# Second feed-forward product in seven block products instead of eight, with 512-column weight tiles and squares on ScalarE

## Chip, cores and metric

The kernel runs on one core of one Trainium2 chip. The metric is the device time of one execution in microseconds (us). The engines are TensorE (PE; its weight loads have a row of their own, PEld), VectorE (DVE), ScalarE (ACT), GpSimd (POOL) and SyncE (SP), the last of which issues most DMA transfers.

## The reference, cut to what matters

A decoder trunk of two layers: 512 tokens plus 16 meta tokens, model width 1024. Each layer is a token mixer (stick-breaking attention, latent attention and retention, joined by one output projection), a layer norm, a feed-forward block and another layer norm:

```python
def squared_relu_mlp(h, w1, w2):
    return jnp.square(jax.nn.relu(h @ w1)) @ w2
...
    for l in range(DEPTH):
        mix = hybrid_mixer(...)
        h = layer_norm(DN_ALPHA * h + mix, ln1_g[l], ln1_b[l])
        h = layer_norm(DN_ALPHA * h + squared_relu_mlp(h, w_ff1[l], w_ff2[l]), ln2_g[l], ln2_b[l])
    return h[:, N_PAD + N_META:]
```

w1 is 1024 x 4096 and w2 is 4096 x 1024, all in float32. The last layer needs only the 512 tokens.

## The kernel before, in words

Activations lie feature-major: a tile has 128 features on the partitions and the tokens on the free axis, 528 tokens in the first layer (layer 0) and 512 in the second (layer 1). Every float32 operand of a product is split into a high part, rounded to the type fp32r by a copy on ScalarE, and a low part, the rest, by a subtraction on VectorE. A 128-deep slice of a product is three matmuls: high x high, high x low, low x high (`proj`, line 554). So an output tile of 128 features over a depth of 1024 takes 24 matmuls for each group of tokens. `groups` (line 563) gives two groups, of 256 and 272 tokens, in layer 0 and one of 512 in layer 1; around layer norms both layers use two halves.

Weights come by `wload` (line 537): one DMA on SP brings 512 KB (128 x 1024) into a raw tile, ScalarE copies it to the high tile and VectorE subtracts to the low tile, in pieces of 512 columns. All three are tiles of one pool W, of ten tiles of 1024 columns (line 436). Other working tiles are units of 528 columns, 63 of them. PSUM has eight banks, shared by two streams of the program.

The feed-forward block (`layer`, from line 1320) works through the 4096 hidden features in four quarters of 1024. In a quarter, `ff1` (line 1324) makes eight tiles of hidden features: product, relu on ScalarE, square on VectorE (which reads PSUM and the relu), split. Then `ff2` (line 1338) makes eight output tiles from those eight hidden ones, and `accum` (line 1238) adds each from PSUM into the running sum r on VectorE; in the first quarter it also brings in the scaled residual, in two instructions. In a layer 24 of the 32 `ff2` output tiles lie in the first three quarters.

At two places in each layer the work is arranged so that a layer norm lies beside matmuls: the last four weights of the mixer's output projection (`nw=4`) and of the last quarter's `ff2` (`nf=4`) are all loaded and held, the first half of the tokens is finished with all of them, and while the second half is multiplied with the same weights the layer norm of the first half runs (`ln_group`, line 639).

The order of the work is not that of the code. All operations are recorded with a rank (`nc.rank`), and a planner (`schedule`, line 314) places them one at a time at the earliest start that its fixed costs give; ties go by rank and then by the order of recording. Each engine then runs its list strictly in that order. A tile of a pool can be given out only when all earlier ones of its stream still fit (`fits`, line 187).

Of the kernel before, what the change touches and what calls it, by code (L numbers as in the profile page):

```python
# [8 lines left out]
F32 = mybir.dt.float32  # L9
F32R = mybir.dt.float32r  # L10
# [5 lines left out]
P = 128  # L16
# [28 lines left out]
def f32(ap):  # L45
    return ap.bitcast(F32)
# [381 lines left out]
class Builder:  # L428
    def __init__(self, ctx, tc, a):
        self.tc, self.a = tc, a  # L430
        self.nc = Recorder(tc.nc)
        self.sb = ctx.enter_context(tc.tile_pool(name="sb", bufs=1))
        self.psp = ctx.enter_context(tc.tile_pool(name="ps", bufs=1, space=bass.MemoryType.PSUM))
        ka, km = PR['KA'], PR['KM']
        self.U = Pool(self.sb, "u", NT, 63).stream(63)
        self.W = Pool(self.sb, "w", 1024, 10).stream(10)
        self.VC = Pool(self.sb, "v", 1280, 3).stream(3)
        self.TC = Pool(self.sb, "t", 48, 12).stream(12)
        ps = Pool(self.psp, "ps", 512, 8)
        self.PA, self.PM = ps.stream(ka), ps.stream(km)  # L440
        self.PP = self.PA
# [95 lines left out]
    def wload(self, src, eng=None):  # L537
        nc = self.nc
        n = src.shape[1]
        raw = self.W.tile([P, 1024], F32)  # L540
        with nc.rank(nc.cur + PR['wd']):
            nc.sync.dma_start(raw[:, :n], src)
        wh = self.W.tile([P, 1024], F32R)
        wl = self.W.tile([P, 1024], F32R)
        with nc.rank(nc.cur + PR['wl']):
            for c in range(0, n, PR['wa']):
                e = min(n, c + PR['wa'])
                nc.scalar.copy(wh[:, c:e], raw[:, c:e])
            for c in range(0, n, PR['wc']):
                e = min(n, c + PR['wc'])  # L550
                (eng or nc.vector).tensor_sub(wl[:, c:e], raw[:, c:e], f32(wh[:, c:e]))
        return wh, wl

    def proj(self, out, w, b0, rhs, c0, c1):
        wh, wl = w
        n = len(rhs)
        for i, (h, l) in enumerate(rhs):
            s = slice((b0 + i) * P, (b0 + i + 1) * P)
            self.mm(out, wh[:, s], h[:, c0:c1], i == 0, False)
            self.mm(out, wh[:, s], l[:, c0:c1], False, False)  # L560
            self.mm(out, wl[:, s], h[:, c0:c1], False, i == n - 1)

    def groups(self, full):
        return self.halves(True) if full else [(0, NX)]
# [22 lines left out]
    def norm_tokens(self, src, xn, n, final=False):  # L587

        nc = self.nc
        st = self.small(16)  # L590
        nc.vector.bn_stats(st[:n, 0:6], src[0])
        nc.vector.bn_stats(st[:n, 6:12], src[1])
        nc.vector.bn_aggr(st[:n, 12:14], st[:n, 0:12])
        self.rstd(st[:n, 14:15], st[:n, 13:14], n)
        if final:
            for i in range(2):
                s = slice(512 * i, 512 * i + 512)
                nc.vector.scalar_tensor_tensor(out=xn[i], in0=src[i], scalar=st[:n, 12:13], in1=self.fg[:n, s],
                                               op0=ALU.subtract, op1=ALU.mult)
                nc.vector.scalar_tensor_tensor(out=xn[i], in0=xn[i], scalar=st[:n, 14:15], in1=self.fb[:n, s],  # L600
                                               op0=ALU.mult, op1=ALU.add)
            return
        nc.vector.scalar_tensor_tensor(out=st[:n, 15:16], in0=st[:n, 12:13], scalar=-1.0, in1=st[:n, 14:15],
                                       op0=ALU.mult, op1=ALU.mult)
        nc.scalar.activation(xn[0], src[0], AF.Identity, bias=st[:n, 15:16], scale=st[:n, 14:15])
        nc.vector.tensor_scalar(out=xn[1], in0=src[1], scalar1=st[:n, 12:13], scalar2=st[:n, 14:15],
                                op0=ALU.subtract, op1=ALU.mult)
# [640 lines left out]
    def layer(self, l, h, first):  # L1248
# [69 lines left out]

        r_mix, r = r, [None] * KT
        nf = PR['nf']  # L1320
        for qd in range(4):
            us, ws3 = [], {}

            def ff1(mt, c0, c1):
                n = c1 - c0
                if mt not in ws3:
                    ws3[mt] = self.wload(self.a["wff1"][l, 8 * qd + mt])
                    us.append((self.unit(F32R), self.unit(F32R)))
                u = us[mt]
                ps = self.mmb()  # L1330
                self.proj(ps[:, :n], ws3[mt], 0, h, c0, c1)
                rl = self.unit()[:, :n]
                nc.scalar.activation(rl, ps[:, :n], AF.Relu)
                sq = self.unit()[:, :n]
                nc.vector.scalar_tensor_tensor(out=sq, in0=ps[:, :n], scalar=0.0, in1=rl, op0=ALU.max, op1=ALU.mult)
                self.split(u[0][:, c0:c1], u[1][:, c0:c1], sq, "a")

            def ff2(mt, w, c0, c1):
                n = c1 - c0
                ps = self.mmb()  # L1340
                self.proj(ps[:, :n], w, 0, us, c0, c1)
                self.accum(ps[:, :n], r[mt][:, c0:c1], h[mt] if qd == 0 else None, c0, c1)

            head = PR['head'] if qd == 0 else 0
            for mt in range(head):
                ff1(mt, *gs[0])
            if qd == 0:
                with nc.rank(R + 23):
                    self.ln_group(r_mix, 1 + 2 * l, hn, *gs[1], False)
            for mt in range(head):  # L1350
                ff1(mt, *gs[1])
            for mt in range(head, 8):
                for g in gl:
                    ff1(mt, *g)
            for mt in range(8 if qd < 3 else 8 - nf):
                w = self.wload(self.a["wff2"][l, qd, mt])
                if qd == 0:
                    r[mt] = self.unit()
                for g in gl:
                    ff2(mt, w, *g)  # L1360
        final = l == DEPTH - 1
        ws = {mt: self.wload(self.a["wff2"][l, 3, mt]) for mt in range(8 - nf, 8)}
        for i, g in enumerate(gs):
            with nc.rank(R + 30 + 2 * i):
                for mt in range(8 - nf, 8):
                    ff2(mt, ws[mt], *g)
        if final:
            self.fg = self.W.tile([P, 1024], F32)
            self.fb = self.W.tile([P, 1024], F32)
            nc.sync.dma_start(self.fg, self.a["fgb"][:, 0:1024])  # L1370
            nc.sync.dma_start(self.fb, self.a["fgb"][:, 1024:2048])
        hn = None if final else self.new_h()
        with nc.rank(R + 31):
            self.ln_group(r, 2, hn, *gs[0], final)
# [117 lines left out]
def _arrays(x, meta_tokens, ln_emb_g, ln_emb_b, w_in, mla_q_norm, mla_kv_norm, w_uq, w_ukv, w_out,  # L1492
            ln1_g, ln1_b, w_ff1, w_ff2, ln2_g, ln2_b):
    A = lambda v: np.asarray(v)
    d = _tables()
    d["xm"] = np.concatenate([A(x)[0][::-1], A(meta_tokens)[::-1]], 0)

    def chunks(w, tiles):

        L, K = w.shape[:2]  # L1500
        v = w[:, :, tiles.reshape(-1)].reshape(L, K // P, P, tiles.shape[0], P)
        return np.ascontiguousarray(v.transpose(0, 3, 2, 1, 4)).reshape(L, tiles.shape[0], P, K)

    d["win"] = chunks(A(w_in), _win_cols())
    uq = chunks(A(w_uq), _uq_cols().reshape(8, P)).reshape(DEPTH, 4, 2, P, 384)
    d["wuq"] = uq.transpose(0, 1, 3, 2, 4).reshape(DEPTH, 4, P, 768)
    ukv = chunks(A(w_ukv), _ukv_cols().reshape(8, P)).reshape(DEPTH, 4, 2, P, 256)
    d["wukv"] = ukv.transpose(0, 1, 3, 2, 4).reshape(DEPTH, 4, P, 512)
    wo = A(w_out).reshape(DEPTH, 3, 4, P, 4, 2, P)
    d["wout"] = wo[:, [0, 2, 1]].transpose(0, 1, 4, 3, 5, 2, 6).reshape(DEPTH, 3, 4, P, 1024)  # L1510
    d["wff1"] = chunks(A(w_ff1), np.arange(D_FF).reshape(32, P))
    f2 = A(w_ff2).reshape(DEPTH, 4, 8, P, 8, P)
    d["wff2"] = f2.transpose(0, 1, 4, 3, 2, 5).reshape(DEPTH, 4, 8, P, 1024)
    col = lambda v: A(v).reshape(-1, P).T
    sets = [(ln_emb_g, ln_emb_b), (A(ln1_g)[0], A(ln1_b)[0]), (A(ln2_g)[0], A(ln2_b)[0]), (A(ln1_g)[1], A(ln1_b)[1])]
    sm = [np.concatenate([col(g), col(b)], 1) for g, b in sets]
    for l in range(DEPTH):
        sm += [col(A(mla_q_norm)[l]), col(A(mla_kv_norm)[l])]
    d["csmall"] = np.concatenate(sm, 1)
    d["fgb"] = np.broadcast_to(np.concatenate([A(ln2_g)[1], A(ln2_b)[1]])[None], (P, 2048))  # L1520
    return {n: np.ascontiguousarray(v) for n, v in d.items()}
# [16 lines left out]
```

## Time and profile before

| | us |
|---|---|
| median of 3 runs (1598.54 to 1599.52) | 1598.9 |
| profiled execution, its own time | 1599.59 |
| its span, first to last instruction | 1597.6 |

The profile is of one execution. Busy time of PE is that of matmuls that overlap each other, so it says that PE had work, not how fast it went; the rate is read from counts of matmuls in a stretch. Mean durations of single instructions hold a latency that the next instruction overlaps, so the rate of an engine is read from stretches in which instructions follow each other without a gap. All instructions have one line (416), since the planner issues them all from there; they are told apart by tiles (u: working units, w: weights, ps: PSUM, t: small ones).

### The profile page before, as it was taken

The page shows a single profiled execution, that of the slowest core. Times are in us where ns is not written, and L with a number is a line of the kernel's source. Part 1 is how long each engine was busy: PE and PEld are TensorE (multiplying, and loading weights), DVE is VectorE, ACT ScalarE, POOL GpSimd, SP SyncE. Part 2 cuts the span into 40 slices and gives each one's busy share as a digit, 9 for nine tenths or more (in the row PEclk, how much of TensorE's full clock was granted, in tenths as well). Part 3 has the DMA queues.
Part 4 walks back from the last instruction along what each step waited for, and adds up shares of the span by engine and source line. Part 5 has one row for each costly group of instructions (what it writes and reads, how often), then busy time and mean ns, then how long its engine had stood idle before and what let it go on. Part 6 is the DMA issues. An engine that isn't in the chain of part 4 may idle for free.

```text
span 1597.6 us, 27869 instructions
## 1 busy us (share of the span) xinstructions
PE 1564.4 (98%) x10842; PEld 1454.4 (91%) x10842; DVE 1038.0 (65%) x2549; ACT 768.2 (48%) x1787; POOL 103.7 (6%) x201
## 2 busy tenths in 40 slices
PE   6999999999999999999999999999999999999997
PEld 6999999988999999999999999988889888888887
DVE  7777777899784443434467767869998544344445
ACT  5664744588553241423336666545885414232330
POOL 5112100110000000000002112001000000000000
PEclk9999999999999999999999999999999999999999
DMA  5423422312122222222224223323112332223332
GB/s 201 111 72 110 128 74 77 93 59 61 52 82 94 93 93 89 85 92 93 93 67 133 84 77 106 115 78 113 57 55 66 107 100 97 92 93 93 98 99 79
DMA packets 46627, 146.23 MB, mean 92 GB/s; under 512 B 7328, under 2 KB 7584, under 8 KB 46496
## 3 DMA queue, kind: packets, MB, share of 16 engines
q1 hardware_dynamic: 41376, 130.46, 25.9%
q0 software_dynamic: 5120, 14.00, 3.5%
q8 instruction: 85, 1.39, 0.4%
q14 instruction: 46, 0.38, 0.1%
HBM read 124.05 MB, written 2.10 MB: 79 GB/s over the span
## 4 chain that ended last, share of the span: by engine, by line
PE 89%; DVE 6%; ACT 3%; issue 1%; DMA 1%; SPq 0%; POOL 0%; DVEq 0%; ACTq 0%
PE ps L416 89%; DVE u L416 4%; ACT u L416 3%; DVE t L416 2%; DVE w L416 1%; DMA w<-in_win 0%; DMA u<-u 0%; ACT w L416 0%; SPq L416 0%; POOL u L416 0%; DVE v L416 0%; ACT t L416 0%; DVEq L1533 0%; ACTq L416 0%; DVEq L416 0%
## 5 line engine op out<-in xcount | busy, mean ns | idle before, releaser
L416 PE MATMUL ps<-u,w 128*128 128x256 f32 (+2 forms) x8736 | 1342.2, 311 | 4.0 <-DVE u L416 4.0
L416 PEld LDWEIGHTS ps<-u,w 128*128 128x128 f32 x8736 | 1209.3, 189 | 88.0 <-DVE u L416 3.3
L416 ACT CAST w<-w 128x512 fp32r<-128x512 f32 (+1 forms) x448 | 257.5, 617 | 299.7 <-DMA w<-in_wff 259.8
L416 DVE TENSOR_TENSOR w<-w,w 128x512 fp32r<-128x512 f32 (+1 forms) x442 | 291.5, 682 | 168.9 <-PE ps L416 156.4
L416 DVE TENSOR_TENSOR u<-u,u 128x256 fp32r<-128x256 f32 (+10 forms) x422 | 218.5, 537 | 60.0 <-ACT u L416 57.9
L416 ACT ACTIVATE u<-ps 128x256 f32<-128x256 f32 (+7 forms) x237 | 114.4, 488 | 174.1 <-PE ps L416 157.9
L416 ACT CAST u<-u 128x256 fp32r<-128x256 f32 (+5 forms) x226 | 112.9, 505 | 143.6 <-DVE u L416 133.4
L416 DVE TENSOR_TENSOR u<-u,ps 128x256 f32<-128x256 f32 (+2 forms) x132 | 62.6, 479 | 147.8 <-PE ps L416 147.5
L416 DVE SCALAR_TENSOR_TENSOR u<-ps,u 128x256 f32<-128x256 f32 (+8 forms) x172 | 91.7, 537 | 67.0 <-ACT u L416 66.3
L416 DVE TENSOR_TENSOR u<-ps,u 128x16 fp32r<-128x16 f32 (+12 forms) x312 | 114.7, 402 | 25.1 <-ACT u L416 19.1
L416 PE MATMUL ps<-ident,u 128*128 128x128 f32 x672 | 102.4, 278 | 12.6 <-DVE t L416 10.3
L416 PE MATMUL ps<-u,u 128*128 128x512 f32 (+4 forms) x528 | 103.1, 314 | 0.0
L416 PEld LDWEIGHTS ps<-ident,u 128*128 128x128 f32 x672 | 80.5, 143 | 18.6 <-DVE u L416 9.2
L416 PE MATMUL ps<-u,v 128*128 128x400 f32 (+4 forms) x484 | 90.0, 301 | 3.5 <-ACT u L416 2.0
L416 POOL DMA_DIRECT2D u<-u x112 | 57.8, 522 | 485.6 <-ACT u L416 445.8
L416 ACT ACTIVATE u<-u 128x512 f32<-128x512 f32 (+5 forms) x146 | 76.2, 546 | 16.1 <-DVE u L416 14.6
L416 PEld LDWEIGHTS ps<-u,u 128*128 128x128 f32 x528 | 79.5, 190 | 2.7
L416 PEld LDWEIGHTS ps<-u,v 128*128 128x128 f32 x484 | 72.7, 189 | 9.6 <-ACT u L416 3.8
L416 ACT COPY u<-ps 128x256 f32<-128x256 f32 (+5 forms) x108 | 43.5, 416 | 47.7 <-PE ps L416 46.7
L416 ACT CAST u<-ps 128x16 fp32r<-128x16 f32 (+7 forms) x188 | 49.3, 335 | 25.0 <-PE ps L416 19.0
L416 ACT ACTIVATE u<-ps,t 128x512 f32<-128x512 f32 (+4 forms) x86 | 47.9, 563 | 18.5 <-DVE t L416 16.7
L416 DVE CAST u<-u 128x256 fp32r<-128x256 f32 (+5 forms) x147 | 50.7, 361 | 8.4 <-ACT u L416 7.8
(64 smaller groups left out, 640.2 us busy)
## 6 DMA issues: line engine op xcount, KB each, us to landing
w<-in_wff SPq DMA_DIRECT2D x128, 512.0 KB, 3.5
w<-in_win SPq DMA_DIRECT2D x60, 512.0 KB, 3.8
w<-in_wout SPq DMA_DIRECT2D x24, 512.0 KB, 3.6
u<-u POOLq DMA_DIRECT2D x80, 132.0 KB, 4.2
u<-u SPq DMA_DIRECT2D x48, 66.0 KB, 2.2
w<-in_wuq SPq DMA_DIRECT2D x8, 384.0 KB, 3.1
u<-in_xm SPq DMA_DIRECT2D x10, 256.0 KB, 6.1
u<-in_dec SPq DMA_DIRECT2D x8, 264.0 KB, 3.9
```

The costliest lines, as they stand in the source:

```text
L416: o.ins = getattr(getattr(nc, o.eng), o.fn)(*[r(x) for x in o.args], **{k: r(x) for k, x in o.kw.items()})
```

## The change

In three of the four quarters of each layer `ff2` is replaced by `strassen`. The 2 x 2 block form takes two output tiles at a time (m = 0 to 3 in a quarter), splits the depth of 1024 into two halves of 512 and the tokens into two halves of H columns (H = 264 in layer 0, 256 in layer 1). Seven products of 12 matmuls with H columns replace eight of them. The weights of the seven products are four blocks of 128 x 512 and three sums: s1 and s3 are made by a plain load and a second load from GpSimd that adds into the tile, s2 and s4 by additions on VectorE. The right-hand sides are likewise four blocks and three differences, made once for each quarter by `strassen_inputs` from pairs of hidden tiles. Results are added to r or subtracted from it after each product: seven additions where there were four. Between the end of `ff1` of a quarter and its block products, the first tile of the next quarter's `ff1` is placed. The last quarter of each layer stays as it was.

In those three quarters the square goes from VectorE to ScalarE; in the last quarter too. Raw weights get a pool of their own, R, of eight tiles with 512 columns; W becomes fourteen tiles of 512 columns, for high and low parts alone. Each weight of 1024 columns is now two DMAs of 256 KB. The norm's constants of the last layer become four tiles of 512 columns. The host lays the w2 of three quarters out by blocks; the numbers in it are the same.

```diff
-        self.W = Pool(self.sb, "w", 1024, 10).stream(10)
+        self.W = Pool(self.sb, "w", 512, 14).stream(14)
+        self.R = Pool(self.sb, "r", 512, 8).stream(8)
...
     def wload(self, src, eng=None):
...
-        raw = self.W.tile([P, 1024], F32)
+        out = []
+        for c in range(0, n, 512):
+            e = min(n, c + 512)
+            raw = self.R.tile([P, e - c], F32)
+            with nc.rank(nc.cur + PR['wd']):
+                nc.sync.dma_start(raw, src[:, c:e])
+            hi, lo = self.wsplit(raw, eng)
+            out += [(hi[:, i:i + P], lo[:, i:i + P]) for i in range(0, e - c, P)]
+        return out
+
+    def wsplit(self, raw, eng=None):
...
+        hi, lo = self.W.tile([P, n], F32R), self.W.tile([P, n], F32R)
+        with nc.rank(nc.cur + PR['wl']):
+            nc.scalar.copy(hi, raw)
+            (eng or nc.vector).tensor_sub(lo, raw, f32(hi))
+        return hi, lo
+
+    def strassen_weights(self, l, qd, m):
...
+        nc, src = self.nc, self.a["wf2"][l, qd, m]
+        a11, a12, a21, a22 = (src[:, i:i + 512] for i in range(0, 2048, 512))
+        t = {}
         with nc.rank(nc.cur + PR['wd']):
...
+            for name, first, more in (("a12", a12, ()), ("s1", a21, (a22,)), ("a11", a11, ()), ("s3", a21, (a11,)),
+                                      ("a22", a22, ())):
+                t[name] = self.R.tile([P, 512], F32)
+                nc.sync.dma_start(t[name], first)
+                for x in more:
+                    nc.gpsimd.dma_start(t[name], x, accum_op=ALU.add)
+        w = {}
+        for name in ("a12", "a11", "s1", "s2", "s4", "s3", "a22"):
+            if name in ("s2", "s4"):
+                x, y = ("s1", "a11") if name == "s2" else ("s2", "a12")
+                t[name] = self.R.tile([P, 512], F32)
+                nc.vector.tensor_add(t[name], t[x], t[y])
+            w[name] = self.wsplit(t[name])
+        return w
+
+    def strassen_inputs(self, x, e, eh, el):
...
+        t3, t4, t2, t1 = t[:, :H], t[:, H:2 * H], e, b12
+        nc.vector.tensor_sub(t3, b22, b12)
+        nc.vector.tensor_sub(t1, b11, b12)
+        nc.vector.scalar_tensor_tensor(out=t2, in0=t3, scalar=-1.0, in1=b11, op0=ALU.mult, op1=ALU.subtract)
+        nc.vector.scalar_tensor_tensor(out=t4, in0=t2, scalar=-1.0, in1=b21, op0=ALU.mult, op1=ALU.subtract)
+        d = {}
+        for x, names in ((b, ("b21", "b22")), (a, ("b11", "t1")), (e, ("t2",)), (t, ("t3", "t4"))):
+            n = H * len(names)
+            hi, lo = (eh, el) if x is e else (self.unit(F32R)[:, :n], self.unit(F32R)[:, :n])
+            self.split(hi, lo, x[:, :n], "a")
...
+        def ff1(qd, mt, c0, c1):
...
+            nc.scalar.activation(rl, ps[:, :n], AF.Relu)
+            if qd == 3:
+                nc.scalar.activation(rl, rl, AF.Square)
+                self.split(us[qd][mt][0][:, c0:c1], us[qd][mt][1][:, c0:c1], rl, "a")
+                return
+            x = raw[qd][mt]
+            nc.scalar.activation(x[:, c0:c1], rl, AF.Square)
...
+        def strassen(qd, m):
+            w = self.strassen_weights(l, qd, m)
...
+            X, Y, Z = (self.mmb()[:, :H] for _ in range(3))
...
+            prod(Y, "a12", "b21", True, True)
+            add(Y, 0, 0)
+            prod(X, "a11", "b11", True, False)
+            add(X, 0, 0)
+            prod(Z, "s1", "t1", True, False)
+            add(Z, 1, 1, ALU.subtract)
+            prod(X, "s2", "t2", False, False)
+            add(X, 0, 1)
+            prod(Z, "s4", "b22", False, True)
+            add(Z, 0, 1)
+            prod(X, "s3", "t3", False, False)
+            add(X, 1, 1, ALU.subtract)
+            prod(X, "a22", "t4", False, True)
+            add(X, 1, 0, ALU.subtract)
+
+        order1 = [0, 4, 1, 5, 2, 6, 3, 7]
         for qd in range(4):
...
+            if qd < 3:
                 for g in gl:
-                    ff2(mt, w, *g)
+                    ff1(qd + 1, 0, *g)
+                for m in range(4):
+                    strassen(qd, m)
```

`prod` is the loop over four slices of 128, three matmuls each; `add` adds one PSUM bank into r on VectorE, in the first quarter with one more instruction for each of the four blocks of r.

## Rows read from the trace of the kernel before

**Rows 1.** The page: span, and busy time of each engine.

```profile
span 1597.6 us, 27869 instructions
PE 1564.4 (98%) x10842; PEld 1454.4 (91%) x10842; DVE 1038.0 (65%) x2549; ACT 768.2 (48%) x1787; POOL 103.7 (6%) x201
```

**Rows 2.** Who PE waited for, whole run: total us, times, longest us.

```profile
PE ps L416 <- DVE t L416: 10.3, 2, 8.1
PE ps L416 <- DVE u L416: 6.2, 11, 2.2
PE ps L416 <- ACT u L416: 5.2, 8, 1.5
```

**Rows 3.** Busy time by stretch: start, feed-forward of layer 0, of layer 1.

```profile
0.00:20.00 20.00, 9.10 (x48) 8.11 (x49) 14.64 (x45) 10.19 (x23) 10.78 (x16) 0.91 0.93 331
...
500.00:800.00 300.00, 300.00 (x2465) 300.00 (x2465) 132.22 (x268) 95.70 (x200) 2.13 (x4) 1.00 0.29 90
1260.00:1560.00 300.00, 300.00 (x1298) 243.59 (x1297) 125.78 (x197) 95.04 (x163) 0.00 (x0) 1.00 0.30 95
```

Its columns: stretch, length, busy us (instructions) of PE, PEld, DVE, ACT, POOL, then granted clock, DMA share, GB/s.

**Rows 4.** Matmul groups by form, stretches 500:800 and 1260:1560: xcount | busy, mean ns.

```profile
L416 PE MATMUL ps<-u,w 128*128 128x272 f32 x1241 | 164.0, 288 | 0.0
L416 PE MATMUL ps<-u,w 128*128 128x256 f32 x1224 | 153.0, 281 | 0.0
...
L416 PE MATMUL ps<-u,w 128*128 128x512 f32 x1298 | 300.5, 394 | 0.0
```

**Rows 5.** Timeline at the end, PEld and DVE: start us, us, instructions.

```profile
1573.10 11.40 PEld L416 LDWEIGHTS ps<-u,w 128*128 128x128 f32 x96
...
1584.44 1.78 PEld L416 LDWEIGHTS ps<-ident,u 128*128 128x128 f32 x16
...
1584.75 0.42 DVE L416 TENSOR_TENSOR u<-u,ps 128x256 f32<-128x256 f32 x1 [2.40 <-PE ps L416]
```

**Rows 6.** Timeline, three stretches without a gap on DVE or ACT.

```profile
419.95 1.14 ACT L416 CAST w<-w 128x512 fp32r<-128x512 f32 x2
...
422.00 1.42 DVE L416 TENSOR_TENSOR u<-u,ps 128x256 f32<-128x256 f32 x4 [1.21 <-PE ps L416]
...
1555.36 1.29 DVE L416 TENSOR_TENSOR w<-w,w 128x512 fp32r<-128x512 f32 x2
```

**Rows 7.** Groups by form: DVE and ACT in 500:800, the last of the whole run.

```profile
L416 DVE TENSOR_TENSOR w<-w,w 128x512 fp32r<-128x512 f32 x102 | 67.4, 688 | 63.7 <-PE ps L416 63.7
L416 ACT CAST w<-w 128x512 fp32r<-128x512 f32 x104 | 59.2, 617 | 119.1 <-DMA w<-in_wff 114.6 <-DVE u L416 4.4
...
L416 DVE SCALAR_TENSOR_TENSOR u<-ps,u 128x256 f32<-128x256 f32 x24 | 10.2, 425 | 19.1 <-ACT u L416 19.1
...
L416 ACT CAST u<-u 128x256 fp32r<-128x256 f32 x24 | 9.8, 407 | 11.8 <-DVE u L416 11.8
...
L416 ACT ACTIVATE u<-ps 128x256 f32<-128x256 f32 x24 | 9.2, 384 | 27.7 <-PE ps L416 27.7
...
L416 ACT ACTIVATE u<-u 128x256 f32<-128x256 f32 x18 | 7.5, 417 | 3.4 <-DVE u L416 3.1
```

**Rows 8.** DMA issues: KB each, median us from issue to landing.

```profile
w<-in_wff SPq DMA_DIRECT2D x128, 512.0 KB, 3.5
...
u<-u POOLq DMA_DIRECT2D x80, 132.0 KB, 4.2
...
w<-in_wukv SPq DMA_DIRECT2D x8, 256.0 KB, 2.6
...
u<-u POOLq DMA_DIRECT2D x16, 66.0 KB, 3.1
```

**Rows 9.** Timeline at the first layer norm of layer 0, between the token halves.

```profile
428.28 1.77 PEld L416 LDWEIGHTS ps<-ident,u 128*128 128x128 f32 x16
...
441.58 0.77 DVE L416 TENSOR_TENSOR u<-u,u 128x256 fp32r<-128x256 f32 x2
...
444.10 2.13 PE L416 MATMUL ps<-ident,u 128*128 128x128 f32 x18
```

More of the change, by code (lines that the diff above doesn't have):

```diff
@@ L539, in wload @@
         n = src.shape[1]
-        raw = self.W.tile([P, 1024], F32)
-        with nc.rank(nc.cur + PR['wd']):
[L542 to L551, printed above, removed]
@@ L552, in wload @@
-        return wh, wl
+        out = []
[8 more added lines that the diff above has]
+    def wsplit(self, raw, eng=None):
+        nc = self.nc
+        n = raw.shape[1]
+        hi, lo = self.W.tile([P, n], F32R), self.W.tile([P, n], F32R)
[3 more added lines that the diff above has]
+        return hi, lo
@@ new lines, in strassen_inputs @@
+    def strassen_inputs(self, x, e, eh, el):
+        nc = self.nc
+        a, b = x
+        H = e.shape[1]
+        t = self.unit()
+        b11, b12, b21, b22 = a[:, :H], a[:, H:2 * H], b[:, :H], b[:, H:2 * H]
+        t3, t4, t2, t1 = t[:, :H], t[:, H:2 * H], e, b12
[8 more added lines that the diff above has]
+            self.split(hi, lo, x[:, :n], "a")
+            for i, k in enumerate(names):
+                d[k] = (hi[:, i * H:i * H + H], lo[:, i * H:i * H + H])
+        return d
@@ L554, in proj @@
     def proj(self, out, w, b0, rhs, c0, c1):
-        wh, wl = w
         n = len(rhs)
         for i, (h, l) in enumerate(rhs):
[L558 to L561, printed above, removed]
+            wh, wl = w[b0 + i]
+            self.mm(out, wh, h[:, c0:c1], i == 0, False)
+            self.mm(out, wh, l[:, c0:c1], False, False)
@@ L563, in groups @@
+            self.mm(out, wl, h[:, c0:c1], False, i == n - 1)
     def groups(self, full):
@@ L596, in norm_tokens @@
             for i in range(2):
-                s = slice(512 * i, 512 * i + 512)
-                nc.vector.scalar_tensor_tensor(out=xn[i], in0=src[i], scalar=st[:n, 12:13], in1=self.fg[:n, s],
+                nc.vector.scalar_tensor_tensor(out=xn[i], in0=src[i], scalar=st[:n, 12:13], in1=self.fgb[i][:n],
                                                op0=ALU.subtract, op1=ALU.mult)
-                nc.vector.scalar_tensor_tensor(out=xn[i], in0=xn[i], scalar=st[:n, 14:15], in1=self.fb[:n, s],
+                nc.vector.scalar_tensor_tensor(out=xn[i], in0=xn[i], scalar=st[:n, 14:15], in1=self.fgb[2 + i][:n],
                                                op0=ALU.mult, op1=ALU.add)
@@ L1320, in layer @@
         nf = PR['nf']
-        for qd in range(4):
[L1322 to L1342, printed above, removed]
+        NQ = NT if full else NX
@@ new lines, in layer @@
+        H = NQ // 2
+        us, ws3 = [[] for _ in range(4)], [{} for _ in range(4)]
+        raw = [{} for _ in range(4)]
+        half = [None]
+        def ff1(qd, mt, c0, c1):
+            n = c1 - c0
+            if mt not in ws3[qd]:
+                ws3[qd][mt] = self.wload(self.a["wff1"][l, 8 * qd + mt])
+                if qd == 3:
+                    us[qd].append((self.unit(F32R), self.unit(F32R)))
+                else:
+                    raw[qd][mt] = self.unit()
+            ps = self.mmb()
+            self.proj(ps[:, :n], ws3[qd][mt], 0, h, c0, c1)
+            rl = self.unit()[:, :n]
+            nc.scalar.activation(rl, ps[:, :n], AF.Relu)
+            if qd == 3:
+                nc.scalar.activation(rl, rl, AF.Square)
[3 more added lines that the diff above has]
+            nc.scalar.activation(x[:, c0:c1], rl, AF.Square)
+            if c1 == NQ and mt >= 4:
+                i = mt - 4
+                if i % 2 == 0:
+                    half[0] = self.unit(F32R), self.unit(F32R)
+                c = slice((i % 2) * H, (i % 2) * H + H)
+                us[qd].append(self.strassen_inputs((raw[qd][i], x), self.unit()[:, :H], half[0][0][:, c], half[0][1][:, c]))
@@ new lines, in ff2, with prod, add @@
+        def ff2(qd, mt, w, c0, c1):
+            n = c1 - c0
+            ps = self.mmb()
+            self.proj(ps[:, :n], w, 0, us[qd], c0, c1)
+            self.accum(ps[:, :n], r[mt][:, c0:c1], None, c0, c1)
+        def strassen(qd, m):
+            w = self.strassen_weights(l, qd, m)
+            if qd == 0:
+                for mt in (2 * m, 2 * m + 1):
+                    r[mt] = self.unit()
+            X, Y, Z = (self.mmb()[:, :H] for _ in range(3))
+            touched = set()
+            def prod(ps, wk, uk, first, last):
+                wh, wl = w[wk]
+                for i in range(4):
+                    b = slice(i * P, i * P + P)
+                    uh, ul = us[qd][i][uk]
+                    self.mm(ps, wh[:, b], uh, first and i == 0, False)
+                    self.mm(ps, wh[:, b], ul, False, False)
+                    self.mm(ps, wl[:, b], uh, False, last and i == 3)
+            def add(ps, row, col, op=ALU.add):
+                mt, c = 2 * m + row, slice(col * H, col * H + H)
+                o = r[mt][:, c]
+                if qd == 0 and (row, col) not in touched:
+                    touched.add((row, col))
+                    nc.vector.scalar_tensor_tensor(out=o, in0=f32(h[mt][0][:, c]), scalar=ALPHA, in1=ps, op0=ALU.mult, op1=op)
+                    nc.vector.scalar_tensor_tensor(out=o, in0=f32(h[mt][1][:, c]), scalar=ALPHA, in1=o, op0=ALU.mult, op1=ALU.add)
+                else:
+                    nc.vector.tensor_tensor(o, o, ps, op=op)
+            prod(Y, "a12", "b21", True, True)
[12 more added lines that the diff above has]
+            add(X, 1, 0, ALU.subtract)
@@ L1344, in layer @@
+        order1 = [0, 4, 1, 5, 2, 6, 3, 7]
+        for qd in range(4):
+            seq = order1 if qd < 3 else list(range(8))
             head = PR['head'] if qd == 0 else 0
-            for mt in range(head):
-                ff1(mt, *gs[0])
+            for mt in seq[:head]:
+                ff1(qd, mt, *gs[0])
             if qd == 0:
@@ L1349, in layer @@
                     self.ln_group(r_mix, 1 + 2 * l, hn, *gs[1], False)
-            for mt in range(head):
-                ff1(mt, *gs[1])
-            for mt in range(head, 8):
+            for mt in seq[:head]:
+                ff1(qd, mt, *gs[1])
+            for mt in seq[max(head, 1 if qd else 0):]:
                 for g in gl:
[L1354 to L1358, printed above, removed]
-                for g in gl:
-                    ff2(mt, w, *g)
+                    ff1(qd, mt, *g)
+            if qd < 3:
+                for g in gl:
+                    ff1(qd + 1, 0, *g)
+                for m in range(4):
+                    strassen(qd, m)
+            else:
+                for mt in range(8 - nf):
+                    w = self.wload(self.a["wff2"][l, 0, mt])
+                    for g in gl:
+                        ff2(qd, mt, w, *g)
         final = l == DEPTH - 1
-        ws = {mt: self.wload(self.a["wff2"][l, 3, mt]) for mt in range(8 - nf, 8)}
+        ws = {mt: self.wload(self.a["wff2"][l, 0, mt]) for mt in range(8 - nf, 8)}
         for i, g in enumerate(gs):
@@ L1365, in layer @@
                 for mt in range(8 - nf, 8):
-                    ff2(mt, ws[mt], *g)
+                    ff2(3, mt, ws[mt], *g)
         if final:
[L1368 to L1371, printed above, removed]
+            self.fgb = [self.W.tile([P, 512], F32) for _ in range(4)]
+            for i in range(4):
+                nc.sync.dma_start(self.fgb[i], self.a["fgb"][:, 512 * i:512 * i + 512])
         hn = None if final else self.new_h()
@@ L1513, in _arrays @@
     d["wff2"] = f2.transpose(0, 1, 4, 3, 2, 5).reshape(DEPTH, 4, 8, P, 1024)
+    f2 = d["wff2"][:, :3].reshape(DEPTH, 3, 4, 2, P, 1024)
+    d["wf2"] = f2.transpose(0, 1, 2, 4, 3, 5).reshape(DEPTH, 3, 4, P, 2048)
+    d["wff2"] = d["wff2"][:, 3:]
     col = lambda v: A(v).reshape(-1, P).T
```

## The prediction, made before the changed kernel ran

> **What bounds the kernel now.** I read the page first: TensorE is busy for 98% of the span, VectorE for 65%, ScalarE for 48% [rows 1]. A busy share says only that matmuls were under way, so next come the waits: in the whole run PE waits 21.7 us for others, 8.1 us of it in a single wait [rows 2]. Then the stretches: between 500 and 800 us, inside the feed-forward block of layer 0, and between 1260 and 1560 us, in that of layer 1, PE has no idle time, at full granted clock, while VectorE is busy for 44% and 42% and ScalarE for 32% [rows 3]. There the time is the number of matmuls times their pace. So what this change is worth is the matmuls that it takes out, less every wait that it brings into a stretch which has none.
>
> The pace comes from counts. In layer 0 there are 2465 matmuls in 300 us, 256 and 272 columns in equal parts [rows 3, 4]: 121.7 ns for 264 columns on average, and H is 264 there. In layer 1 there are 1298 of 512 columns: 231.1 ns. H = 256 in layer 1 has its own row: 96 of 256 columns from 1573.10 to 1584.44 us [rows 5], 118.1 ns.
>
> **The change part by part.**
>
> *Matmuls.* Before, a quarter's second product took 8 tiles x 24 matmuls x 2 groups = 384 in layer 0 and 192 in layer 1; the block form takes 4 x 7 x 12 = 336 of H columns in both. Layer 0: (384 - 336) x 121.7 ns = 5.84 us a quarter. Layer 1: 192 x 231.1 = 44.4 us against 336 x 118.1 = 39.7 us, 4.69 us a quarter. Three quarters of each: 17.5 + 14.1 = **31.6 us off PE's path**. The first products keep their matmuls.
>
> Layer 1 gains less because it trades 512 columns for 256, and weight loads become as many as in layer 0, where PEld is busy for all 300 us against 243.6 [rows 3]. The 118.1 ns already contain that. The Trainium skill (TensorE: Matmul & The Clock Gate, section Back-to-back issue gap) gives a sustained pace of about 81 ns at 128 columns and 131 ns at 512. A straight line between them makes 98 ns at 256 (an estimate), and then layer 1 would lose 336 x 98 - 192 x 131 = 7.8 us a quarter where the rows give 4.69 us of gain. The trace does not agree with its 512-column figure (231.1 ns).
>
> *VectorE beside the block products.* Instructions that follow each other start 1.29 - 0.69 = 0.60 us apart at 512 columns and (1.42 - 0.42) / 3 = 0.33 us at 256 [rows 6]; what I take off is the duration of a single one [rows 5, 7], whose end overlaps the next. For each m, seven subtractions and two additions of 512 and seven additions from PSUM: 9 x 0.60 + 7 x 0.33 = 7.7 us, beside 84 matmuls, 9.9 us in layer 1 and 10.2 us in layer 0. In a first quarter four more residual instructions make 9.0 us, 91%. It hides, but only just in the first quarters; with single durations instead it would be 9 x 0.69 + 11 x 0.42 = 10.8 us, 0.9 us too long for each of eight m, 7 us in all. ScalarE has seven casts a (1.14 - 0.62) = 0.52 us [rows 6, 7], 3.6 us.
>
> *ScalarE and VectorE beside the first product.* For a hidden tile of layer 0, 48 x 121.7 ns = 5.84 us of PE, ScalarE does two relus (0.384), two squares (0.417 by the nearest row), two weight casts (0.617) and 3.5 input casts of H columns (0.407) [rows 7]: 4.3 us. VectorE loses the squares (0.425 each) and has two weight subtractions, 3.5 input subtractions and two differences: 1.4 + 5.5 x 0.425 = 3.7 us. Both hide. The last pair's chain (relu 0.38, square 0.42, four differences 1.3, subtraction 0.43, and five changes of engine at the 0.31 us of the next part: 4.1 us) has the next quarter's first tile, 5.5 to 5.8 us of PE, as its cover. Without it, 4 us would show in each of six quarters.
>
> *PSUM hand-offs.* X and Z are added to r in the middle of their accumulation, so the next product into the bank waits for VectorE: four such places in each m. The forward way was 0.31 us (the next load at 1584.44, the addition at 1584.75) [rows 5], the addition takes 0.42, the way back has no row and I take 0.31 again: 1.04 us. A product of 12 matmuls lies between, 1.42 us, except after s3, where the next m's first product must be placed. With a 0.69 us instruction on VectorE just begun, 0.31 us shows. Between 0 and 4 x 0.31 us for each of 24 m; I take 0.1 us for each m, near the lower end, as VectorE is free a fifth of the time: **+2.4 us** (0 to 30).
>
> *Weight loads.* Each m brings seven transfers of 256 KB, 1.84 MB in 9.9 us, 185 GB/s; the core took 331 GB/s at the start [rows 3]. A plain 256 KB lands in 2.6 us against 3.5 for 512 KB [rows 8], so halves come no later. SP's queue issues five instead of two, POOL's two, and nothing else waits in POOL's queue there. The adding loads have no row; see the rivals. I take 0.
>
> *Fourteen tiles where sixteen are wanted.* The four held weights at each layer norm now need 4 x 4 = 16 tiles of W and there are 14 (before, 8 of 10). The last half weight can be split only after the second token half has used the first one: 12 matmuls, then cast and subtraction, some 3.4 us late, at four places. What that delays is the layer norm's chain, from the transposes at 428.28 to the last split at 442.35 us; PE had matmuls of the second half until 444.10 [rows 9]. So 1.7 us of slack and then the first product's matmuls, which need the normalised tiles one by one, absorb most. From 0 to 3.4 us each; I take 0.75, because that work starts with the tiles that are ready: **+3 us**.
>
> *The pool in the attention stretches.* Same instructions, but other room: seven weights' worth of raw and split tiles, 2 x 7 + 8 halves, against ten tiles that hold three weights and a third. It changes what the planner places first. Lower end -3 us (part of the waits of 21.7 us); upper +10 us (one in ten of the code's 100 weights there late by a cast and a subtraction, 0.52 + 0.60 us). I take **+2 us**, nearer to nothing.
>
> Sum against the profiled execution's own 1599.6 us (span 1597.6, and 2.0 around it): 1599.6 - 31.6 + 2.4 + 3 + 2 = 1575.4. The median of the runs lies 0.7 us below that execution: **1574.7 us**.
>
> **The rivals.**
>
> *Hand-offs show (0.13).* VectorE's queue is strict, and a weight split or two ahead of an addition from PSUM stops PE at the bank. For: 78 to 91% of VectorE's time is taken. Against: an addition that is ready goes before later splits by rank. At half of the worst case, 0.15 us at 96 places, 14.4 us instead of 2.4: 1587.
>
> *Pools (0.07).* The attention stretches and the four layer norms pay their upper ends, 10 + 4 x 2 = 18 us instead of 5: 1588.
>
> *The adding loads bound the block products: slower (0.08).* Place: pool R. An m needs seven of its eight tiles, so the next m's s1 cannot be loaded before s2 is formed. Round trip: addition 0.60 + plain load 2.6 + adding load A, against 9.9 us. The Trainium skill (DMA: Bandwidth & Descriptors, section Rules for kernel authors) says that an accumulating DMA must wait for the semaphore of the earlier one on the same bytes; no run here shows such a transfer. The first m is loaded during the first product. For m=1 a tile is free when the next quarter's first tile has run 2.2 us of its 5.5 (two splits), and s1 is ready A + 2.6 - 3.4 = A - 0.8 us after the block products begin, and m=3's two round trips later, 5.6 + 3A; it is wanted, a split earlier than its product, at 3 x 9.9 + 1.7 = 31.4 us. So nothing shows until A = 8.6 us, and each quarter gives back its 31.6 / 6 = 5.3 us at A = 10.4 us; at A = 13 us the kernel takes 1575 + 6 x 13.2 = 1654. For: the price is unknown. Against: POOL's transfers land in 3.1 us at 66 KB and 4.2 at 132 KB [rows 8], by size some 6.3 us at 256 KB, and even a third more costs nothing.
>
> *No change (0.04):* A near 10.4 us, or the first two rivals together.
>
> *Weight loads show in layer 1 (0.01).* A quarter there gets 336 - 192 = 144 more of them. If each added its 118.1 ns, 17.0 us, three quarters would lose 51 us: 1626; at 73 ns the gain is gone. Against: 96 matmuls of 256 columns with their loads ran at 118.1 ns in all [rows 5]. The Trainium skill's two figures above point this way, and by them alone it would be 1612 (an estimate).
>
> **How the numbers follow.** The forecast case has 0.67. Faster by over 0.2% (3.2 us, about what can be told from no change) is 0.67 + 0.13 + 0.07 = 0.87; within it 0.04; slower 0.08 + 0.01 = 0.09. The lower end, 1565, has all of the 31.6 us with 2 us gained elsewhere; the upper, 1590, takes in hand-offs at half their price and the pools' upper ends, and leaves out the last three cases and their neighbours.
>
> **What would show it.** Right: 336 matmuls of H columns in each of six quarters at 121.7 and 118.1 ns, no PE wait on VectorE of more than some tenths of a us there, a second feed-forward product shorter by 5 to 6 us a quarter. POOL's adding loads landing in 5 to 8.6 us. PE idle near the layer norms by 1 us or so. Wrong: PE waiting for w or for DVE in each m, VectorE at 95% or more beside the block products, adding loads beyond 8.6 us, or attention stretches longer by more than 10 us.

## Result and profile after

The changed kernel takes **1570.2 us** (median of 4 runs, 1569.99 to 1570.71) against 1598.9 us: ratio 0.9821, 95% interval 0.9804 to 0.9838, 28.7 us less. The forecast was 1574.7 us, from 1565 to 1590.

The page of the changed kernel, span and busy time (in the form of [rows 1]):

```profile
span 1568.9 us, 30040 instructions
PE 1535.4 (98%) x11130; PEld 1448.0 (92%) x11130; DVE 1169.5 (75%) x2791; ACT 880.4 (56%) x1979; POOL 145.9 (9%) x249
```

PE's share has not moved from that of [rows 1], though its work has shrunk; VectorE is up from 65 to 75%, ScalarE from 48 to 56%. A share of the span would tell nothing of the gain. Who PE waited for, whole run, as in [rows 2]:

```profile
PE ps L416 <- DVE t L416: 10.2, 4, 8.4
PE ps L416 <- DVE u L416: 6.8, 8, 2.3
PE ps L416 <- ACT u L416: 3.8, 5, 1.4
```

In all 20.8 us against 21.7: the change brought no wait that this view counts as new. Between 457 and 790 us and between 1224 and 1540 us, where all 24 m of block products lie, the view lists no wait at all. Now three stretches of block products, columns as in [rows 3]: a first quarter of layer 0, a first quarter of layer 1, and the second quarter of layer 1:

```profile
515.00:535.00 20.00, 20.00 (x166) 20.00 (x165) 18.14 (x39) 8.13 (x15) 1.75 (x2) 1.00 0.60 164
...
1272.00:1296.00 24.00, 24.00 (x206) 24.00 (x205) 22.60 (x48) 10.31 (x18) 2.19 (x3) 1.00 0.70 188
...
1352.00:1380.00 28.00, 28.00 (x241) 28.00 (x240) 23.85 (x44) 12.42 (x20) 3.50 (x4) 1.00 0.71 189
```

PE is full at full clock. VectorE is busy for 91%, 94% and 85%, where the working gave 91% for first quarters and 78% for others: nearly full, and it hides all the same. The pace is 20 us / 166 = 120.5 ns at 264 columns and 28 / 241 = 116.2 ns at 256. Two or three matmuls on the edges are counted in, so these are 1 to 1.5% low. From start to start, 288 matmuls of 264 columns from 501.23 us follow each other at 122.1 ns and 324 of 256 columns from 1430.12 us at 117.7 ns, very near the 121.7 and 118.1 ns that were put in. This weighs more than the empty list of waits, because a gap shorter than the 0.28 us that the profile gives a matmul does not show as idle time of PE. The new form of 264 columns, and the large shift from 512 to 256 columns (1920 of 512 before in the whole run), in the groups by form of the whole run:

```profile
L416 PE MATMUL ps<-u,w 128*128 128x256 f32 x4128 | 539.7, 284 | 2.1 <-DVE u L416 2.0
...
L416 PE MATMUL ps<-u,w 128*128 128x512 f32 x1344 | 330.2, 397 | 0.0
...
L416 PE MATMUL ps<-u,w 128*128 128x264 f32 x1008 | 124.2, 284 | 0.0
```

1008 is 3 quarters x 336. And the transfers, as in [rows 8], with the adding loads that had no row before:

```profile
r<-in_wf SPq DMA_DIRECT2D x120, 256.0 KB, 3.1
...
r<-in_wf POOLq DMA_DIRECT2D x48, 256.0 KB, 4.7
```

A, the time of an adding load, is 4.7 us, below the 6.3 us estimated by size and far below the 8.6 us from which it was to show.

Where most of the loss sits is seen at the layer norms. The timeline of the changed kernel, from the last quarter of layer 0 into its norm (PEld, ACT, DVE and PE rows):

```profile
791.74 1.56 PEld L416 LDWEIGHTS ps<-ident,u 128*128 128x128 f32 x14
...
794.96 0.62 ACT L416 CAST w<-r 128x512 fp32r<-128x512 f32 x1 [12.36 <-PE ps L416]
795.61 0.69 DVE L416 TENSOR_TENSOR w<-r,w 128x512 fp32r<-128x512 f32 x1 [1.66 <-ACT w L416]
...
799.19 0.26 PEld L416 LDWEIGHTS ps<-ident,u 128*128 128x128 f32 x2
...
821.21 2.61 PE L416 MATMUL ps<-ident,u 128*128 128x128 f32 x22 [0.44 <-DVE t L416]
824.52 0.39 PE L416 MATMUL ps<-u,w 128*128 128x256 f32 x1 [0.69 <-DVE u L416]
```

Before, 16 transposes went in one run [rows 9]. Now 14 go, and the last two, of the eighth output tile, follow 7.4 us later: ScalarE has waited for PE to give a weight tile back (12.36 us idle, ended by PE), then come cast, subtraction, 12 matmuls, the addition. The norm's chain is late by as much, and at 821 and 824 us PE stands at its results. The same picture of 14 and 2 transposes stands at all four norms.

### The profile page after: what moved, and what is told of

The parts are those of the page before. It is cut to its first block, busy times and chain, and to the rows that moved or that the text cites. A ratio compares the mean times of both kernels' runs of the same rounds, so it can differ in the third digit from the quotient of the medians.

```text
span 1568.9 us, 30040 instructions
## 1 busy us (share of the span) xinstructions
PE 1535.4 (98%) x11130; PEld 1448.0 (92%) x11130; DVE 1169.5 (75%) x2791; ACT 880.4 (56%) x1979; POOL 145.9 (9%) x249
## 4 chain that ended last, share of the span: by engine, by line
PE 92%; DVE 4%; ACT 2%; issue 1%; DMA 0%; SPq 0%; DVEq 0%; ACTq 0%; POOLq 0%
PE ps L416 92%; DVE u L416 2%; ACT u L416 2%; DVE t L416 2%; DVE w L416 0%; DMA r<-in_win 0%; SPq L416 0%; DMA u<-u 0%; ACT w L416 0%; ACT t L416 0%; DVE v L416 0%; DVEq L1646 0%; ACTq L416 0%; DVEq L416 0%; POOLq L416 0%
## 5 line engine op out<-in xcount | busy, mean ns | idle before, releaser
L416 PE MATMUL ps<-u,w 128*128 128x256 f32 (+3 forms) x9024 | 1312.6, 303 | 3.1 <-DVE u L416 2.0
L416 ACT CAST w<-r 128x512 fp32r<-128x512 f32 (+1 forms) x520 | 315.4, 618 | 384.2 <-PE ps L416 352.4
L416 DVE TENSOR_TENSOR w<-r,w 128x512 fp32r<-128x512 f32 (+1 forms) x514 | 350.3, 688 | 179.2 <-ACT w L416 152.4
L416 DVE TENSOR_TENSOR u<-u,u 128x512 fp32r<-128x512 f32 (+11 forms) x467 | 247.1, 552 | 40.2 <-ACT u L416 37.5
L416 ACT CAST u<-u 128x512 fp32r<-128x512 f32 (+6 forms) x247 | 128.8, 540 | 45.9 <-DVE u L416 39.9
L416 DVE TENSOR_TENSOR u<-u,ps 128x256 f32<-128x256 f32 (+3 forms) x220 | 95.4, 436 | 65.0 <-PE ps L416 62.5
L416 DVE TENSOR_TENSOR u<-ps,u 128x16 fp32r<-128x16 f32 (+14 forms) x312 | 115.3, 400 | 21.8 <-ACT u L416 14.6
L416 ACT ACTIVATE u<-u 128x256 f32<-128x256 f32 (+5 forms) x245 | 124.0, 521 | 5.4 <-DVE u L416 1.3
L416 POOL DMA_DIRECT2D r<-in_wf x48 | 42.1, 877 | 588.9 <-DVE w L416 255.8
L416 DVE SCALAR_TENSOR_TENSOR u<-ps,u 128x432 f32<-128x432 f32 (+7 forms) x73 | 41.4, 579 | 27.6 <-ACT u L416 24.9
```

The lines of the kernel that those rows point to most:

```text
L416: o.ins = getattr(getattr(nc, o.eng), o.fn)(*[r(x) for x in o.args], **{k: r(x) for k, x in o.kw.items()})
```

## The experiments

All are edits of the changed kernel. Each median is of that kernel's own runs; ratios are to the kernel before on the same chip.

**e1, block products taken out, pools and squares kept.** In all quarters:

```diff
-            if qd < 3:
-                for g in gl:
-                    ff1(qd + 1, 0, *g)
-                for m in range(4):
-                    strassen(qd, m)
-            else:
-                for mt in range(8 - nf):
+            if True:
+                for mt in range(8 if qd < 3 else 8 - nf):
```

> The changed kernel with the plain second product in all four quarters (384 and 192 matmuls a quarter again); the new pools and the squares on ScalarE stay. My theory (the whole gain is the 31.6 us of matmuls taken out, and pools and squares cost a little): 1599 to 1604 us, at or just above the kernel before. Rival (pools or squares give part of the gain by themselves): below 1596 us.

Measured: 1603.4 us, ratio 1.0027 (1.0017 to 1.0038). Without the block products nothing is gained, and the pools together with the squares lose some 4 us (the kernel before took 1599.3 us beside it). The block products are worth 33.2 us here.

**e2, squares back on VectorE.**

```diff
-            nc.scalar.activation(x[:, c0:c1], rl, AF.Square)
+            nc.vector.scalar_tensor_tensor(out=x[:, c0:c1], in0=ps[:, :n], scalar=0.0, in1=rl, op0=ALU.max, op1=ALU.mult)
```

(and the same in the last quarter)

> Only the squares go back to VectorE (reading PSUM and the relu), block products stay. My theory (VectorE is then at 4.6 us of 5.84 beside a hidden tile, still hidden): within 2 us of 1570.2 us. Rival (the block form needs the squares off VectorE, since differences and splits follow them): 1575 us or more, with PE waiting for u in the first product.

Measured: 1571.2 us, ratio 0.9826 (0.9810 to 0.9842): the same within the intervals. The squares lie beside the matmuls on either engine; that edit is not what the time came from.

**e3, the next quarter's first tile after the block products.**

```diff
-                for g in gl:
-                    ff1(qd + 1, 0, *g)
                 for m in range(4):
                     strassen(qd, m)
+                for g in gl:
+                    ff1(qd + 1, 0, *g)
```

> The next quarter's first hidden tile is recorded after the block products of the quarter instead of before them. My theory (the last pair's chain of 4.1 us then lies open at the start of each quarter's block products): PE idle for 3 to 4 us in each of six quarters, 1588 to 1596 us. Rival (the planner finds other matmuls for PE): no more than 4 us above 1570.2 us.

Measured: 1579.0 us, ratio 0.9874 (0.9859 to 0.9888), 8.8 us slower than the changed kernel: neither theory. The cover is worth 8.8 / 6 = 1.5 us a quarter. The loss does lie there: with PE's matmuls of both traces counted in order, this kernel falls behind by 3.4 us in the feed-forward block of layer 0 and by 5.2 us in that of layer 1. PE's list of this kernel, the order in which the program gives it its matmuls, shows why it is not more; these are its matmuls at the start of the first block products of layer 0, in order:

```
3740 L416 MATMUL ps_7424<-u_7020,w_7188 128x264
...
3748 L416 MATMUL ps_7424<-u_7287,w_7208 128x264
3749 L416 MATMUL ps_7442<-u_7038,w_7247 128x264
3750 L416 MATMUL ps_7442<-u_7058,w_7247 128x264
3751 L416 MATMUL ps_7442<-u_7038,w_7255 128x264
```

Nine matmuls into one bank, then another bank. Three of a product's four depth slices do not need the last pair, so the planner opens three products (banks 7424, 7442, 7460) with nine matmuls each, 27 x 0.12 = 3.2 us, which PE can run during the last pair's chain. The 3.2 us and the 1.5 us that are left make 4.7 us, near the 4.1 us worked out for the chain; but the working took a product as one piece.

**e4, W with 16 tiles**, for two of the working units.

```diff
-        self.U = Pool(self.sb, "u", NT, 63).stream(63)
-        self.W = Pool(self.sb, "w", 512, 14).stream(14)
+        self.U = Pool(self.sb, "u", NT, 61).stream(61)
+        self.W = Pool(self.sb, "w", 512, 16).stream(16)
```

> W with 16 tiles instead of 14, paid for with two of the 63 working units. My theory (the half weight that comes late at each of the four layer norms is the loss of about 3 us that is left): 1566.5 to 1569.5 us, the transposes before the first half's norm in one run of 16 again, no PE idle near 820 us. Rival (those matmuls are hidden anyway, or the two units are missed elsewhere): 1570 us or more.

Measured: 1562.9 us, ratio 0.9773 (0.9759 to 0.9788), 7.3 us below the changed kernel: twice the most that the theory expected, from the edit that it named. All four norms have 16 transposes in one run again.

**e5 and e6, the adding load of s1 made longer.**

```diff
                 for x in more:
                     nc.gpsimd.dma_start(t[name], x, accum_op=ALU.add)
+                    for _ in range(1 if name == "s1" else 0):
+                        nc.gpsimd.dma_start(t[name], self.a["zero"], accum_op=ALU.add)
```

(e6: 2 instead of 1.)

> After the adding load of s1 a second adding load puts a tile of zeros on top, so this step of the chain takes twice the 4.7 us measured in the changed kernel, A = 9.4 us. My theory as worked out ahead (nothing shows up to A = 8.6 us, then three times the excess in each quarter): 2.4 us a quarter, about 1585 us. Rival A (the round trip has more lead than I gave it, as the third m's sum is issued at 517.6 us for a product near 530 us): below 1573 us. Rival B (adding loads are already the bound of the block products): 4.7 us for each of 18 m, 1650 us.

> Two adding loads of zeros after that of s1, A = 14.1 us. My theory: 3 x 14.1 - 25.8 = 16.5 us in each of six quarters, about 1669 us. Rival A (more lead): the point where it starts to show lies between the two runs, and it gives 1575 to 1630 us. Rival B: 1740 us.

Measured: 1573.05 us, ratio 0.9832 (0.9817 to 0.9847), and 1593.2 us, 0.9956 (0.9941 to 0.9971). The second is Rival A's; the first lies at its bound of 1573 us (the four runs took 1572.9 to 1574.0 us), and far from the 1585 us of the theory. In e5 the chain is 4.9 + 4.7 = 9.6 us long by its medians and costs 2.9 us in all; in e6 it is 4.4 + 2 x 5.2 = 14.8 us and costs 23.0 us, 3.8 us a quarter where the working gives 18.6. GpSimd's issues in the first quarter of e6 show the step that failed (timeline, POOL rows):

```profile
487.30 0.87 POOL L416 DMA_DIRECT2D r<-in_wf  x1 [2.80 <-DVE u L416]
491.71 0.87 POOL L416 DMA_DIRECT2D r<-in_zero  x1 [3.54 <-DMA r<-in_wf]
...
497.41 1.23 POOL L416 DMA_DIRECT2D r<-in_zero  x1
```

and who PE waited for in e6 between 460 and 760 us:

```profile
PE ps L416 <- DVE w L416: 6.7, 6, 2.0
```

The second m's sum starts at 487.3 us and is done at about 497.4 + 5.2 = 502.6 us. The first matmul of the block products starts at 501.1 us in this run, so the sum is ready 1.5 us after their start; the working gave A - 0.8 = 14 us. So there are 12.5 us more of lead: the load is issued well before the next quarter's first tile, where the working had it wait for that tile. But the mechanism is there: with a chain long enough, PE waits for w, the split weights.

**e7 and e10, the two sums on VectorE made twice and four times.**

```diff
-                nc.vector.tensor_add(t[name], t[x], t[y])
+                for _ in range(2):
+                    nc.vector.tensor_add(t[name], t[x], t[y])
```

(e10: 4 instead of 2.)

> s2 and s4 are each added twice on VectorE (the second time with the same result), 1.2 us more for each m: 8.9 of 9.9 to 10.2 us, and 10.2 to 10.3 us in the first quarters. My theory (VectorE's work lies beside the matmuls until it is full): 1570 to 1574 us. Rival (PE waits at PSUM banks for additions, and the more so the fuller VectorE's queue is): 0.1 us or more at each of 96 places, 1579 us or more.

> s2 and s4 are each added four times on VectorE, 3.6 us more than in the changed kernel for each m: 11.3 us of work beside 9.9 (layer 1) or 10.2 us, and 12.6 us in the first quarters. My theory (VectorE becomes the bound once it is full): 1.4 and 1.1 us over in eight m of each layer, 2.7 and 2.4 us in four, 40 us in all, less up to 5 us a quarter that weights split ahead absorb: 1580 to 1610 us. Rival (the work of the first product that is planned around it absorbs it too): below 1576 us.

Measured: e7 1571.0 us, ratio 0.9818 (0.9803 to 0.9833), and e10 1591.4 us, 0.9943 (0.9926 to 0.9960). The first quarter of layer 1, first e7, then e10:

```profile
1272.00:1296.00 24.00, 23.97 (x202) 23.67 (x201) 23.50 (x50) 10.29 (x19) 2.63 (x3) 1.00 0.60 158
```

```profile
1272.00:1296.00 24.00, 23.18 (x193) 22.63 (x191) 23.34 (x49) 8.09 (x15) 2.63 (x3) 1.00 0.46 121
```

Both lie in the range of the theory. At 98% of the stretch in e7 VectorE costs PE almost nothing (0.8 us in all; of its 202 matmuls three have 512 columns, and 288 of 256 columns from 1261.26 us start 118.9 ns apart, where they were 118.0 ns apart in the changed kernel), so the additions from PSUM do not hold PE up: the hand-off rival falls. With 3.6 us more for each m VectorE is the bound, and PE gets 193 matmuls through where it got 206 in the changed kernel. VectorE's work hides until it is full, and only then shows; 3.6 us more of it for each m take back 21.2 of the 28.7 us.

**e8, two tiles for the late half weight alone.** W keeps 14; the last half of the fourth held weight goes to a pool of its own:

```diff
+        self.W2 = Pool(self.sb, "x", 512, 2).stream(2)
...
-        hi, lo = self.W.tile([P, n], F32R), self.W.tile([P, n], F32R)
+        pool = self.W2 if self.extra else self.W
+        hi, lo = pool.tile([P, n], F32R), pool.tile([P, n], F32R)
...
+            self.extra = held and c > 0
             hi, lo = self.wsplit(raw, eng)
+            self.extra = False
```

(`held` is set for output tile 7 of `ff2` and chunk 3 of the output projection; units are 61.)

> W stays at 14 tiles; two more tiles (paid for with two working units) serve only the last half weight of the four held at each layer norm. My theory (the 7 us that 16 tiles gave come from the late half weight at the layer norms): 1562 to 1565 us. Rival (they come from the room in the attention stretches): 1568 us or more.

Measured: **1562.2 us**, ratio 0.9767 (0.9750 to 0.9783), 8.0 us below the changed kernel and as good as e4. Attention has the 14 tiles of the changed kernel. The same place of its timeline as above (PEld rows; x is the new pool):

```profile
788.38 1.50 PEld L416 LDWEIGHTS ps<-u,x 128*128 128x128 f32 x12
789.83 1.77 PEld L416 LDWEIGHTS ps<-ident,u 128*128 128x128 f32 x16
```

The twelve matmuls of the half weight come ahead of the transposes, and all 16 go at once.

**e9, e1 with the two tiles of e8.** The edits of both.

> The plain second product in all four quarters (as in the first run) with the two extra tiles for the last held half weight. My theory (the pools' only cost is the late half weight at the four layer norms): 1595 to 1598 us, 6 to 8 us below the first run, so that the block products against their own plain form are worth 33 to 35 us in both pairs. Rival (the half weight is late only because the block products come before it): 1601 us or more.

Measured: 1594.6 us, ratio 0.9956 (0.9941 to 0.9971), 8.8 us below e1, 0.4 us under the range of the theory. The late half weight costs about the same with and without block products (8.8 and 8.0 us), so the rival falls. Between e9 and e8 the second product's form differs, with the order of the hidden tiles that goes with it: 32.4 us, a little less than the 33 to 35 us expected. The two ran on different chips, beside which the kernel before took 1601.2 us (e9) and 1599.6 us (e8); taken by the ratios the difference is 30.2 us. The medians are the better measure here: beside e9, five of the seven runs of the kernel before had a granted clock of 0.994 or 0.995, and the two at 0.996 took 1598.4 and 1599.9 us, while all four runs of e9 had 0.998.

**e11, W with 18 tiles**, U with 59 units (the edit of e4 with other numbers).

> W with 18 tiles, paid for with four of the 63 working units. My theory (16 are what the layer norms need, more room does nothing): within 2 us of the 1562.5 us of 16 tiles. Rival (the block products too gain from more weights split ahead): 1560 us or less. If four units are missed: 1566 us or more.

Measured: 1565.6 us, ratio 0.9777 (0.9763 to 0.9792), 2.7 us above e4: outside the 2 us of the theory and just short of the 1566 us of missed units. Room beyond 16 tiles gives nothing; whether the four units are missed or the plan only falls out otherwise was not tried.

## Why the prediction was right, and where its terms were off

The mechanism was as forecast, and the sizes of three small terms were not. The starts of the transposes before the norms cut the span into stretches; these are their lengths in four kernels, whose transposes go in one run of 16 or, in the changed kernel, of 14 (there a half weight's twelve matmuls, 1.4 us, are still to come):

| us | to the norm in layer 0 | feed-forward 0 | mixer of layer 1 | feed-forward 1 | rest |
|---|---|---|---|---|---|
| before | 428.3 | 383.2 | 396.5 | 363.4 | 26.2 |
| after (14) | 425.6 | 366.1 | 398.8 | 350.0 | 28.3 |
| e9, plain | 425.7 | 382.3 | 395.4 | 363.8 | 25.7 |
| e8, block products | 424.8 | 365.1 | 395.2 | 349.2 | 25.7 |

*Matmuls, -31.6 us: right.* From e9 to e8 the feed-forward blocks shrink by 17.3 and 14.6 us, where the counts gave 17.5 and 14.1. The runs say 32.4 us. The step from 512 to 256 columns did not cost more than its row (117.7 ns against 118.1): the rival of the weight loads falls, and with it the 1612 us. The trace of after stands against the Trainium skill's 131 ns at 512 columns as that of before did: 187 matmuls of 512 columns from 1386.82 us start 231.5 ns apart (TensorE: Matmul & The Clock Gate, section Back-to-back issue gap).

*VectorE and ScalarE beside the matmuls, 0: right.* VectorE is at 91 to 94% in stretches of first quarters, PE has no wait there, and e2 and e7 are within 1 us.

*Hand-offs, +2.4 us: too much.* There is no wait in the block products, their pace is that of plain matmuls, and e7 with VectorE at 98% loses 0.8 us. The working put one product between an addition and the bank's next use. e3's list shows that PE may have three products open at once, which leaves a late addition more time; that this is the reason was not tried.

*Weight loads and adding loads, 0: right.* An adding load takes 4.7 us, just under the 5 to 8.6 us that the prediction named as its sign. A plain half took 3.1 us and not 2.6, and PE did not wait for one. The threshold of 8.6 us was put too low, as e5's 9.6 us cost 2.9 us in all; e6 shows the step, the lead of the second m.

*Fourteen tiles, +3 us: too small, measured +8.0.* The step said "12 matmuls, then cast and subtraction, some 3.4 us late". Left out were the 14 transposes that now come in between, the late twelve matmuls themselves and the addition: 7.4 us from the first transposes to the last two. And it took the norm's chain as absorbed for the most part; 8.0 us over four places would be 2.0 each, about halfway between the 0.75 taken and the upper end of 3.4. Where the time goes is less even. With PE's matmuls of the two traces counted in order, the changed kernel falls behind e8 by 0.6, 2.4, 1.1 and 1.1 us across the four norms, and e1 behind e9 by 1.0, 2.3, 2.0 and 1.2 us: 5.2 of 8.9 us and 6.5 of 9.5 us. In both pairs another 1.3 us comes in the 40 us before the first norm and about 1 us in the mixer of layer 1, so the late half weight reaches beyond the norms. PE's waits show only 2.7 us of it (20.8 us against 18.1 in e8).

*The pool in the attention stretches, +2 us: wrong sign, measured -4.3* (e9 against before, 1594.6 against 1598.9; it holds the squares too, which e2 shows to be worth 1.0 at most). The table has it in the stretch up to the first norm (-2.6), the mixer of layer 1 (-1.1) and in small parts elsewhere. What in those stretches became shorter is not shown: no single wait of before is gone from the list. The step also miscounted the room, as seven weights' worth of tiles: fourteen tiles of 512 columns hold the high and low parts of three and a half weights, and the raw ones have their own; before, ten tiles held three and a third in all. And half of the gain comes early: PE's 400th matmul starts at 68.5 us in before and at 66.8 us in e9, and by 150 us e9 is 2.2 us ahead. From 20 to 40 us, first before, then e9:

```profile
20.00:40.00 20.00, 17.82 (x135) 17.64 (x134) 14.82 (x44) 11.41 (x26) 9.26 (x22) 0.91 0.24 72
```

```profile
20.00:40.00 20.00, 18.73 (x154) 18.34 (x154) 17.64 (x48) 12.38 (x28) 11.13 (x24) 1.00 0.45 141
```

The trace of before has a granted clock of 0.91 here and in the first 20 us [rows 3], that of e9 has 1.00 in both. So part of what the table has may be the clock of that one execution, and part of the 4.3 us the start, where the first weights now come in halves; neither was tried. The cause stays open.

So -32.4 + 8.0 - 4.3 = -28.7 us by differences of runs (they add up by construction), where -31.6 + 2.4 + 3 + 2 = -24.2 us was forecast. The main term, and with it the size of the gain, was worked out; that the sum came within 4.5 us of the measured time is in part luck, since two misses of 5 and 6 us have opposite signs.

## What to carry to other kernels

Where one engine is full with nothing to wait for, count the instructions that a change takes out of its list and multiply by the pace of a stretch; that came out within 1 us of 32. Then go through every place where a pool must hold a set of tiles all at once, and count that set in the new tile size: two tiles too few (of 512 columns each) cost 8 us here, a quarter of the gain, and could be paid for with two working units without a loss that the runs show. Do not take a high busy share of another engine as a loss: VectorE at 91 to 98% still hid here, and showed only when its work for each m was longer than the matmuls beside it. Test the margin by doubling a harmless instruction.

## What the runs showed that was not expected

An adding load of 256 KB lands 4.7 us after its issue, against 3.1 us for a plain one of the same size beside it and 3.6 us for GpSimd's 132 KB copies in the same run (medians): less than size had suggested (6.3 us). And VectorE could be busy for 98% of a stretch (e7) without PE losing more than 0.8 us in the whole run.
